# RMSNorm with GELU on one core: gamma replicated on the chip, two rows of each partition per transfer, results written in place

One NeuronCore of a Trainium2 chip. The metric is the device time of the program in microseconds, the median over several executions. All runs told here are fast, with a granted clock of 1.0.

## The reference

```python
# x: 8 x 1024 x 2048 float32, gamma: 2048 float32, eps = 1e-5
rms = np.sqrt(np.mean(x ** 2, axis=-1, keepdims=True) + eps)
out = gamma * x / rms
return 0.5 * out * (1 + np.tanh(np.sqrt(2 / np.pi) * (out + 0.044715 * out ** 3)))
```

The input and the output are 8192 rows of 8 KB, 67.1 MB each. Each row is read once and written once.

## The kernel before

A tile is 128 rows, one for each partition, 1 MB. Eight tiles make a chunk. While a chunk is loaded and its squares are summed (even tiles on ScalarE, odd ones on VectorE), the chunk ahead of it is multiplied by gamma on VectorE, sent through Gelu on ScalarE with 1/rms as the scale, and stored.

```python
P = 128
CHUNK = 8
singles = ctx.enter_context(tc.tile_pool(name="singles", bufs=1))
gamma_bc = singles.tile([P, D], fp32)
nc.gpsimd.dma_start(out=gamma_bc, in_=gamma.partition_broadcast(P))
xpool = ctx.enter_context(tc.tile_pool(name="xp", bufs=16))
ypool = ctx.enter_context(tc.tile_pool(name="yp", bufs=7))
# ... cut: pools of squares and statistics

def emit_load(i, x_tile):
    nc.sync.dma_start(out=x_tile, in_=xf[i * P:(i + 1) * P, :])

def emit_apply(i, x_tile, inv_rms, j):
    y_tile = ypool.tile([P, D], fp32)
    nc.vector.tensor_tensor(out=y_tile, in0=x_tile, in1=gamma_bc, op=ALU.mult)
    nc.scalar.activation(out=y_tile, in_=y_tile, func=AF.Gelu_apprx_tanh,
                         scale=inv_rms[:, j:j + 1])
    nc.gpsimd.dma_start(out=of[i * P:(i + 1) * P, :], in_=y_tile)
# ... cut: emit_sumsq; the loop over chunks; sqrt and reciprocal once a chunk
```

## Time and profile before

| | before |
|---|---|
| time, median | 327.62 us (326.97 to 327.99, 15 runs) |
| span of the profiled execution | 325.5 us |
| busiest engine | VectorE, 217.0 us |
| bytes moved by DMA | 135.32 MB, 416 GB/s over the span |
| transfers of 1 MB | 64 loads, 64 stores, 1 for gamma |

The times of this kernel wander between 326.8 and 328.0. That is why kernels of different sessions are compared here by their ratios to it.

### The profile page before, as it was taken

Reading aid. Unit: us, or ns where it says so; the run is one execution under the profiler, and the core shown is the slowest. Engines: PE = TensorE matmul, PEld = TensorE weight load, DVE = VectorE, ACT = ScalarE, POOL = GpSimd, SP = SyncE. Lnnn points to the kernel's source line nnn. Section 1 sums busy time; section 2 is a strip of 40 time slices with the busy share of each in tenths; the row PEclk is TensorE's granted clock in tenths of the full one; section 3 lists DMA queues with packets and bytes.
Section 4 is the critical chain, followed back from the end, with each engine's and each line's share of the span. In section 5 each row is a group of like instructions: output and inputs, shape, how many; then the busy total and the mean of one; then the engine's idle time right before and its main releaser. Section 6 shows DMA issues by size and latency. Waiting matters only on the chain.

```text
span 325.5 us, 723 instructions
## 1 busy us (share of the span) xinstructions
DVE 217.0 (67%) x137; ACT 208.1 (64%) x153; POOL 34.9 (11%) x69
## 2 busy tenths in 40 slices
DVE  0599722866667767766668768766668677699800
ACT  4230599519993139936994269925796398685940
POOL 1000012101110001110111002110111001110210
DMA  7999999999999999999999999999999999999994
GB/s 298 427 422 423 423 412 429 426 429 426 429 426 425 430 424 430 426 428 428 428 427 427 427 428 429 424 430 426 429 426 429 426 428 426 426 428 391 413 406 200
DMA packets 18582, 135.32 MB, mean 416 GB/s; under 512 B 2064, under 2 KB 2064, under 8 KB 2064
## 3 DMA queue, kind: packets, MB, share of 16 engines
q0 software_dynamic: 9360, 68.16, 49.8%
q1 hardware_dynamic: 9216, 67.11, 49.2%
q14 instruction: 6, 0.05, 0.0%
HBM read 68.16 MB, written 67.11 MB: 416 GB/s over the span
## 4 chain that ended last, share of the span: by engine, by line
issue 65%; DMA 10%; POOL 9%; DVE 6%; ACT 5%; POOLq 0%; DVEq 0%; PEldq 0%; ACTq 0%
POOL out_dram L78 9%; DMA out_dram<-y_tile 7%; DVE y_tile L73 4%; DMA gamma_bc<-in_gamma_dram 3%; ACT y_tile L74 3%; DVE sq_v L64 2%; ACT sq_s L58 1%; ACT L74 0%; ACT L108 0%; POOLq L78 0%; POOLq L145 0%; ACT rms L108 0%; DVE inv_rms L113 0%; DVE sumsq L64 0%; DVEq L73 0%
## 5 line engine op out<-in xcount | busy, mean ns | idle before, releaser
L73 DVE TENSOR_TENSOR y_tile<-x_tile,gamma_bc 128x2048 f32<-128x2048 f32 x64 | 145.7, 2290 | 88.8 <-DMA out_dram<-y_tile 73.4
L74 ACT ACTIVATE y_tile<-y_tile,inv_rms 128x2048 f32<-128x2048 f32 x64 | 124.6, 1990 | 30.3 <-DVE inv_rms L113 21.0
L64 DVE CUSTOM_DVE_ANT_0 sq_v<-x_tile 128x2048 bf16<-128x2048 f32 x32 | 73.0, 2281 | 0.0
L58 ACT ACTIVATE sq_s<-x_tile 128x2048 bf16<-128x2048 f32 x32 | 60.7, 1895 | 15.2 <-DMA x_tile<-in_x_dram 15.2
L78 POOL DMA_DIRECT2D out_dram<-y_tile x64 | 34.0, 531 | 277.5 <-ACT y_tile L74 277.5
L108 ACT ACT_TABLE_LOAD x8 | 10.3, 1283 | 47.5 <-DVE sumsq L64 47.5
L74 ACT ACT_TABLE_LOAD x8 | 10.3, 1283 | 0.1
L108 ACT ACTIVATE rms<-sumsq,eps_t 128x8 f32<-128x8 f32 x8 | 2.4, 301 | 10.8 <-DVE sumsq L64 10.7
L58 ACT ACTIVATION_READ_ACCUMULATOR sq_s<-x_tile 128x1 f32 x32 | 6.0, 186 | 0.0
L113 DVE RECIPROCAL inv_rms<-rms 128x8 f32<-128x8 f32 x8 | 1.6, 198 | 1.7 <-ACT rms L108 1.7
L64 DVE DVE_READ_ACCUMULATOR2_ANT sumsq<- 128x1 f32 x32 | 2.6, 83 | 0.0
L58 ACT ACT_TABLE_LOAD x1 | 1.3, 1283 | 0.7 <-PEq L131 0.7
L39 POOL DMA_DIRECT2D gamma_bc<-in_gamma_dram x1 | 0.7, 667 | 0.8 <-PEq L145 0.8
L41 DVE MEMSET eps_t<- 128x1 f32 x1 | 0.1, 59 | 0.8 <-PEq L131 0.8
L131 POOL MEMSET const-float32-0.0<- 128x1 f32 x1 | 0.1, 98 | 0.2 <-issue 0.2
L131 POOL MEMSET const-bfloat16-1.0<- 128x1 bf16 x1 | 0.1, 101 | 0.0
L131 POOL MEMSET const-uint8-127<- 128x1 uint8 x1 | 0.1, 99 | 0.0
L131 POOL MEMSET const-float32-1.0<- 128x1 f32 x1 | 0.1, 98 | 0.0
## 6 DMA issues: line engine op xcount, KB each, us to landing
x_tile<-in_x_dram SPq DMA_DIRECT2D x64, 1024.0 KB, 28.0
out_dram<-y_tile POOLq DMA_DIRECT2D x64, 1024.0 KB, 18.2
gamma_bc<-in_gamma_dram POOLq DMA_DIRECT2D x1, 1024.0 KB, 10.3
```

The costliest lines, as they stand in the source:

```text
L39: nc.gpsimd.dma_start(out=gamma_bc, in_=gamma.partition_broadcast(P))
L41: nc.vector.memset(eps_t, eps_f)
L58: nc.scalar.activation(out=sq_s, in_=x_tile, func=AF.Square, accum_out=sumsq[:, j:j + 1],)
L64: nc.vector.tensor_tensor_reduce(out=sq_v, in0=x_tile, in1=x_tile, scale=1.0, scalar=0.0, op0=ALU.mult, op1=ALU.add, accum_out=sumsq[:, j: ...
L73: nc.vector.tensor_tensor(out=y_tile, in0=x_tile, in1=gamma_bc, op=ALU.mult)
L74: nc.scalar.activation(out=y_tile, in_=y_tile, func=AF.Gelu_apprx_tanh, scale=inv_rms[:, j:j + 1],)
L78: nc.gpsimd.dma_start(out=of[i * P:(i + 1) * P, :], in_=y_tile)
L108: nc.scalar.activation(out=rms[:, :cn], in_=sumsq[:, :cn], func=AF.Sqrt, bias=eps_t, scale=1.0 / D,)
L113: nc.vector.reciprocal(out=inv_rms[:, :cn], in_=rms[:, :cn])
L131: nc = _bacc.Bacc("TRN2", target_bir_lowering=False, num_devices=1)
```

## The change

Its intent: to move fewer bytes and to move them in larger pieces. Gamma is read once as a row of 8 KB and replicated into PSUM by matmuls with a column of ones, in place of a broadcast load of 1 MB. A block is 256 rows, of which partition p holds rows 2p and 2p+1, contiguous in memory on both sides: 16 KB per partition, 2 MB per transfer. The results overwrite the block, so there are no y tiles; 11 blocks take the place of 16 x tiles and 7 y tiles. The multiply takes both rows at once, and only the very last block's is split.

```diff
-    CHUNK = 8
+    SUB = 2
+    CHUNK = 4
+    xb = xf.rearrange("(b p s) d -> b p s d", p=P, s=SUB)
+    ob = of.rearrange("(b p s) d -> b p s d", p=P, s=SUB)
-    gamma_bc = singles.tile([P, D], fp32)
-    nc.gpsimd.dma_start(out=gamma_bc, in_=gamma.partition_broadcast(P))
+    gamma_row = singles.tile([1, D], fp32)
+    nc.scalar.dma_start(out=gamma_row, in_=gamma.partition_broadcast(1))
+    ones = singles.tile([1, P], fp32)
+    nc.vector.memset(ones, 1.0)
+    gamma_bc = psum.tile([P, D], fp32)
+    for n in range(0, D, 512):
+        nc.tensor.matmul(gamma_bc[:, n:n + 512], ones, gamma_row[:, n:n + 512],
+                         start=True, stop=True)
-    xpool = ctx.enter_context(tc.tile_pool(name="xp", bufs=16))
-    ypool = ctx.enter_context(tc.tile_pool(name="yp", bufs=7))
+    xpool = ctx.enter_context(tc.tile_pool(name="xp", bufs=11))
-        nc.sync.dma_start(out=x_tile, in_=xf[i * P:(i + 1) * P, :])
+                blk = xpool.tile([P, SUB, D], fp32)
+                nc.sync.dma_start(out=blk, in_=xb[b])
-        nc.vector.tensor_tensor(out=y_tile, in0=x_tile, in1=gamma_bc, op=ALU.mult)
+            nc.vector.tensor_tensor(
+                out=blk, in0=blk,
+                in1=gamma_bc[:, None, :].to_broadcast([P, SUB, D]), op=ALU.mult)
+            for s in range(SUB):
+                nc.scalar.activation(
+                    out=blk[:, s, :], in_=blk[:, s, :], func=AF.Gelu_apprx_tanh,
+                    scale=inv_rms[:, 2 * j + s:2 * j + s + 1])
-        nc.gpsimd.dma_start(out=of[i * P:(i + 1) * P, :], in_=y_tile)
+        nc.gpsimd.dma_start(out=ob[b], in_=blk)
 # cut: row 0 of a block is summed on ScalarE, row 1 on VectorE; the split of the
 # last block's multiply; renamed lists and the widths of the statistics' tiles
```

More of the change, by code (lines that the diff above doesn't have):

```diff
@@ L30 @@
     N, D = xf.shape
-    assert N % P == 0
-    ntiles = N // P
-    nchunks = (ntiles + CHUNK - 1) // CHUNK
+    rows_per_block = P * SUB
+    assert N % rows_per_block == 0
+    nblocks = N // rows_per_block
+    nchunks = (nblocks + CHUNK - 1) // CHUNK
+    xb = xf.rearrange("(b p s) d -> b p s d", p=P, s=SUB)
+    ob = of.rearrange("(b p s) d -> b p s d", p=P, s=SUB)
     eps_f = float(eps)
     singles = ctx.enter_context(tc.tile_pool(name="singles", bufs=1))
-    gamma_bc = singles.tile([P, D], fp32)
-    nc.gpsimd.dma_start(out=gamma_bc, in_=gamma.partition_broadcast(P))
+    gamma_row = singles.tile([1, D], fp32)
+    nc.scalar.dma_start(out=gamma_row, in_=gamma.partition_broadcast(1))
+    ones = singles.tile([1, P], fp32)
+    nc.vector.memset(ones, 1.0)
+    psum = ctx.enter_context(tc.tile_pool(name="ps", bufs=1, space=bass.MemoryType.PSUM))
+    gamma_bc = psum.tile([P, D], fp32)
+    for n in range(0, D, 512):
+        nc.tensor.matmul(gamma_bc[:, n:n + 512], ones, gamma_row[:, n:n + 512],
+                         start=True, stop=True)
     eps_t = singles.tile([P, 1], fp32)
     nc.vector.memset(eps_t, eps_f)
-    xpool = ctx.enter_context(tc.tile_pool(name="xp", bufs=16))
-    ypool = ctx.enter_context(tc.tile_pool(name="yp", bufs=7))
+    xpool = ctx.enter_context(tc.tile_pool(name="xp", bufs=11))
     sq_s_pool = ctx.enter_context(tc.tile_pool(name="sqs", bufs=1))
@@ L47 @@
     statpool = ctx.enter_context(tc.tile_pool(name="statp", bufs=3))
-    chunk_x_tiles = {}
+    chunk_blocks = {}
     chunk_inv_rms = {}
-    def emit_load(i, x_tile):
-        nc.sync.dma_start(out=x_tile, in_=xf[i * P:(i + 1) * P, :])
-    def emit_sumsq(j, x_tile, sumsq):
-        if j % 2 == 0:
-            sq_s = sq_s_pool.tile([P, D], bf16)
-            nc.scalar.activation(
-                out=sq_s, in_=x_tile, func=AF.Square,
-                accum_out=sumsq[:, j:j + 1],
-            )
-        else:
-            sq_v = sq_v_pool.tile([P, D], bf16)
-            nc.vector.tensor_tensor_reduce(
-                out=sq_v, in0=x_tile, in1=x_tile,
-                scale=1.0, scalar=0.0,
-                op0=ALU.mult, op1=ALU.add,
-                accum_out=sumsq[:, j:j + 1],
-            )
@@ L71, in emit_apply, with emit_sumsq @@
-    def emit_apply(i, x_tile, inv_rms, j):
-        y_tile = ypool.tile([P, D], fp32)
-        nc.vector.tensor_tensor(out=y_tile, in0=x_tile, in1=gamma_bc, op=ALU.mult)
-        nc.scalar.activation(
-            out=y_tile, in_=y_tile, func=AF.Gelu_apprx_tanh,
-            scale=inv_rms[:, j:j + 1],
-        )
-        nc.gpsimd.dma_start(out=of[i * P:(i + 1) * P, :], in_=y_tile)
+    def emit_sumsq(blk, j, sumsq):
+        sq_s = sq_s_pool.tile([P, D], bf16)
+        nc.scalar.activation(
+            out=sq_s, in_=blk[:, 0, :], func=AF.Square,
+            accum_out=sumsq[:, 2 * j:2 * j + 1],
+        )
+        sq_v = sq_v_pool.tile([P, D], bf16)
+        nc.vector.tensor_tensor_reduce(
+            out=sq_v, in0=blk[:, 1, :], in1=blk[:, 1, :],
+            scale=1.0, scalar=0.0,
+            op0=ALU.mult, op1=ALU.add,
+            accum_out=sumsq[:, 2 * j + 1:2 * j + 2],
+        )
@@ new lines, in emit_apply @@
+    def emit_apply(b, blk, inv_rms, j, split_mult=False):
+        if split_mult:
+            for s in range(SUB):
+                nc.vector.tensor_tensor(
+                    out=blk[:, s, :], in0=blk[:, s, :], in1=gamma_bc,
+                    op=ALU.mult,
+                )
+                nc.scalar.activation(
+                    out=blk[:, s, :], in_=blk[:, s, :], func=AF.Gelu_apprx_tanh,
+                    scale=inv_rms[:, 2 * j + s:2 * j + s + 1],
+                )
+        else:
+            nc.vector.tensor_tensor(
+                out=blk, in0=blk,
+                in1=gamma_bc[:, None, :].to_broadcast([P, SUB, D]), op=ALU.mult
+            )
+            for s in range(SUB):
+                nc.scalar.activation(
+                    out=blk[:, s, :], in_=blk[:, s, :], func=AF.Gelu_apprx_tanh,
+                    scale=inv_rms[:, 2 * j + s:2 * j + s + 1],
+                )
+        nc.gpsimd.dma_start(out=ob[b], in_=blk)
@@ L80 @@
     for c in range(nchunks + 1):
-        cn = min(CHUNK, ntiles - c * CHUNK) if c < nchunks else 0
+        cn = min(CHUNK, nblocks - c * CHUNK) if c < nchunks else 0
         prev = c - 1
-        pn = len(chunk_x_tiles.get(prev, ()))
+        pn = len(chunk_blocks.get(prev, ()))
+        last_chunk = c == nchunks
         if cn > 0:
-            sumsq = statpool.tile([P, CHUNK], fp32)
-            x_tiles = []
+            sumsq = statpool.tile([P, 2 * CHUNK], fp32)
+            blocks = []
@@ L88 @@
             for j in range(cn):
-                i = c * CHUNK + j
-                x_tile = xpool.tile([P, D], fp32)
-                emit_load(i, x_tile)
-                x_tiles.append(x_tile)
-            chunk_x_tiles[c] = x_tiles
+                b = c * CHUNK + j
+                blk = xpool.tile([P, SUB, D], fp32)
+                nc.sync.dma_start(out=blk, in_=xb[b])
+                blocks.append(blk)
+            chunk_blocks[c] = blocks
         for j in range(max(cn, pn)):
             if cn > 0 and j < cn:
-                emit_sumsq(j, chunk_x_tiles[c][j], sumsq)
+                emit_sumsq(chunk_blocks[c][j], j, sumsq)
@@ L98 @@
             if pn > 0 and j < pn:
-                emit_apply(prev * CHUNK + j, chunk_x_tiles[prev][j],
-                           chunk_inv_rms[prev], j)
+                emit_apply(prev * CHUNK + j, chunk_blocks[prev][j],
+                           chunk_inv_rms[prev], j,
+                           split_mult=last_chunk and j == pn - 1)
         if pn > 0:
-            del chunk_x_tiles[prev]
+            del chunk_blocks[prev]
             del chunk_inv_rms[prev]
         if cn > 0:
-            rms = statpool.tile([P, CHUNK], fp32)
+            rms = statpool.tile([P, 2 * CHUNK], fp32)
@@ L108 @@
             nc.scalar.activation(
-                out=rms[:, :cn], in_=sumsq[:, :cn], func=AF.Sqrt,
+                out=rms[:, :2 * cn], in_=sumsq[:, :2 * cn], func=AF.Sqrt,
                 bias=eps_t, scale=1.0 / D,
             )
-            inv_rms = statpool.tile([P, CHUNK], fp32)
-            nc.vector.reciprocal(out=inv_rms[:, :cn], in_=rms[:, :cn])
+            inv_rms = statpool.tile([P, 2 * CHUNK], fp32)
+            nc.vector.reciprocal(out=inv_rms[:, :2 * cn], in_=rms[:, :2 * cn])
```

## The prediction

> **What bounds the kernel now.** I read the page first: the busy shares of the engines, then the DMA lines of the 40 slices.
>
> ```profile
> DVE 217.0 (67%) x137; ACT 208.1 (64%) x153; POOL 34.9 (11%) x69
> DMA  7999999999999999999999999999999999999994
> DMA packets 18582, 135.32 MB, mean 416 GB/s; under 512 B 2064, under 2 KB 2064, under 8 KB 2064
> ```
>
> No compute engine is above 67% over the span, and no slice but the first and the last shows the DMA below 90%. The 16 DMA engines are the bound. To see how exact that is I asked for stretches (columns: start:end, length, busy us of DVE, ACT and POOL, clock, DMA share, GB/s).
>
> ```profile
> 8.00:16.00 8.00, 4.42 (x2) 2.00 (x2) 0.00 (x0) 1.00 1.01 427
> 56.00:280.00 224.00, 157.22 (x100) 152.83 (x114) 25.50 (x48) 1.00 1.01 427
> 299.00:301.00 2.00, 2.00 (x2) 2.00 (x2) 0.53 (x1) 1.00 0.71 299
> 309.00:311.00 2.00, 0.00 (x0) 2.00 (x2) 0.53 (x1) 1.00 1.00 410
> 321.00:323.00 2.00, 0.00 (x0) 0.00 (x0) 0.00 (x0) 1.00 0.09 37
> 323.00:325.50 2.50, 0.00 (x0) 0.00 (x0) 0.00 (x0) 1.00 0.00 0
> ```
>
> The rate is 427 GB/s with loads alone (8 to 16 us) and with loads and stores together (56 to 280), and about 410 with stores alone (309 to 311). The share never falls but for some 1.9 us at the start (0.76 of the first 8 us), 0.6 us around 300 us, and 4.3 us after about 321.2, when the last bytes have landed. So the 325.5 us are about 318.7 us of full DMA and 6.8 us of ends and dip.
>
> The view of waits says who is held, and by what.
>
> ```profile
> DVE y_tile L73 <- DMA out_dram<-y_tile: 73.4, 41, 10.3
> ACT L108 <- DVE sumsq L64: 47.5, 7, 10.8
> DVE y_tile L73 <- DMA gamma_bc<-in_gamma_dram: 10.7, 1, 10.7
> ```
>
> VectorE waits 73.4 us for stores to free y buffers: the engines wait for the transfers. The 10.7 us for gamma are VectorE's, not the DMA's, which ran at 427 GB/s meanwhile. The chain of waits is 65% "issue" and tells little here, as the transfers form a queue that no instruction waits behind. Last, the table of transfers (KB each, median us from issue to landing) and the costs of the instructions:
>
> ```profile
> x_tile<-in_x_dram SPq DMA_DIRECT2D x64, 1024.0 KB, 28.0
> out_dram<-y_tile POOLq DMA_DIRECT2D x64, 1024.0 KB, 18.2
> q1 hardware_dynamic: 9216, 67.11, 49.2%
> L73 DVE TENSOR_TENSOR y_tile<-x_tile,gamma_bc 128x2048 f32<-128x2048 f32 x64 | 145.7, 2290 | 88.8 <-DMA out_dram<-y_tile 73.4
> L74 ACT ACTIVATE y_tile<-y_tile,inv_rms 128x2048 f32<-128x2048 f32 x64 | 124.6, 1990 | 30.3 <-DVE inv_rms L113 21.0
> ```
>
> A load takes 28 us where its own bytes take 2.46 (1.0486 MB at 427 GB/s): with half of the rate each, 28.0/4.9 = 5.7 loads and 18.2/4.9 = 3.7 stores stand in the queues. 9216 packets for 64 loads are 144 a load: 128 rows of 8 KB and 16 small ones.
>
> **What the Trainium skill says.** "DMA: Bandwidth & Descriptors", section "Where 436 GB/s comes from", gives a ceiling of 435.2 GB/s for the 16 engines; this trace holds 427, 98.1% of it. The same page, "Why small descriptors are slow (HBM only)", names a fixed cost of about 3 cycles per packet on trn2; the trace leaves room for such a cost, but doesn't prove it. The same page, "Queues, rings and completion order", says that each DMA engine takes the queues it has work for in turn, packet by packet; the 49.8% and 49.2% of the two queues agree. "VectorE: DVE Perf Modes", "The perf-mode tier table", gives fp32 tensor_tensor one element per cycle from SBUF and from PSUM alike, 2293 ns for 2048 elements; the trace has 2290 from SBUF, and nothing yet from PSUM.
>
> **The change, part by part.**
>
> *Gamma.* The broadcast of 1 MB into 128 partitions goes; one row of 8 KB and four small matmuls into PSUM replace it. As the DMA is full from 3 us on, its 1.0486 MB come off the end: 1.0486/427 = 2.46 us. The matmuls are new and no row prices them; they have until the first block is loaded and summed (2 + 4.9 + 2.3 = some 9 us), and VectorE waited until 11.6 us before anyhow. Nothing on the path.
>
> *Transfers of 2 MB in 16 KB rows.* In the built program both sides are 128 rows of 4096 contiguous floats, so I expect packets of 16 KB: 32 x 144 = 4608 on each queue, half. An 8 KB row takes 8192/(427/16) = 307 ns on its engine; at the page's ceiling it would be 301. If those 6 ns are a cost per packet, halving 1024 data packets on each engine saves 512 x 6 = 3.0 us; if they are the fabric's, nothing. I take half, 1.5 us, an estimate from that page and this trace.
>
> *Vector and scalar work.* 31 multiplies of 4096 elements replace 62 of 2048: by the 2290 ns and 0.96 GHz I estimate 2290 + 2133 = 4.42 us each, so some 5 us of VectorE disappear. A block then costs VectorE 4.4 + 2.28 + 0.08 = 6.8 us and ScalarE 1.9 + 0.19 + 2 x 1.99 = 6.1, against 9.8 us of DMA for a block in and out. All of it beside the DMA: 0.
>
> *Buffers.* 16 x tiles and 7 y tiles become 11 blocks, 22 tiles, written in place; a block is held from its load to the end of its store. Does the DMA stay fed? The multiplies still stand straight after the block's sums in the built order, ahead of the reciprocal. VectorE's chain for the first four blocks: loaded at about 7, then 3 x 6.8 + 2.3 to the last sum, about 30 us; one more multiply, then the reciprocal at 34; two Gelus of 1.99 and the first store at about 38.5 us (43.1 before). Until then only loads run, and 11 blocks last until 2 + 11 x 4.9 = 56 us, so they don't run dry. At 40 us some 7.8 blocks have landed and 3.2 are in the load queue. From there the two queues share the rate, so that number stays. The same reckoning for the kernel before gives 23 tiles less 16.5 at 45 us, 6.5, against the 5.7 read above; I trust it. Four blocks and a bit wait for their chunk, so some 3 blocks stand in the store queue. Full DMA throughout.
>
> *The tail.* After the last load (call it T) the store queue holds about 2.5 blocks, 12.7 us at 412 GB/s. Block 27's store is issued at T + 6.1 (a sum of squares and two Gelus), block 28's at T + 11.2 (last sum 2.4, multiply 4.4, reciprocal 0.2, two Gelus 4.0), then one every 4.0 us against 5.1 of transfer. No gap, so the dip of 0.6 us goes too.
>
> Sum: 327.77 - 2.46 - 0.6 - 1.5 = 323.2 us. I add 0.4 for the first rival below: 323.6.
>
> **Rivals.**
>
> *A gap in the tail.* If the store queue holds only one block at T, it is empty at T + 3, and block 27's bytes start at about T + 7.5: 4.5 us of idle DMA, and all gains but those of the packets are gone, about 327.7. For it: 2 MB stores come in lumps of two Gelus, and every chunk's first Gelu waits for the next load on ScalarE's queue. Against it: the reckoning of the queues. I give a sizeable gap about 1 in 6.
>
> *Starved loads.* In place, a load waits for a store, where before it waited for a multiply. If loads fall behind for 1 us in each of 8 chunks, the time is about 332. Against: 3 blocks of reserve, 30 us at half rate.
>
> *The packets count in full or more.* If bigger rows lift the rate to the ceiling and the stores alone from 412 too, 3 us and about 1 more come: 320.5. For: half as many completions. Against: at 98.1% of the ceiling there is little left.
>
> *PSUM as an operand slows VectorE.* Even at 7 us a multiply the block costs 9.4 us, just below the 9.8: no change in the middle, some 3 us in the tail. The page speaks against it.
>
> **Range and chances.** The gamma term is near certain (2.46); the packets give 0 to 4, the tail takes 0 to 4.5. All good: 320.5. Packets 0 and most of the gap: 327.5. So 320.6 to 327.0 for 8 in 10, at the centre 323.6. Faster by over 2% needs less than 321.2, only the packets' full worth does it: 0.14. Slower by over 2% needs more than 334.3, a starved DMA beyond what the reserve allows: 0.03. Within 2%: 0.83.
>
> **What would show it.** Right: bytes 134.3 MB; packets about 9,200 with none between 512 B and 16 KB but gamma's; share 1.0 from 3 us to the end of the stores; middle rate between 427 and 432; first store issued near 38 us; multiplies at 4.4 us; VectorE's longest wait no more for y tiles. Wrong: a middle rate below 427 (then large rows are worse, and my packet term has the wrong sign), slices below 9 in the middle (starved loads), or a dip of over 2 us some 35 us before the end (the tail's gap).

## The result, and the profile after

The kernel after takes **319.58 us** (319.37 to 319.78, 8 runs), 0.9757 of the time before (95% interval 0.9748 to 0.9766). A ratio is the mean time of one kernel's fast runs over the mean of the other's fast runs of the same rounds, so it isn't quite the ratio of the medians quoted. Predicted were 323.6 us and a range of 320.6 to 327.0. The direction was right, the size was not: 8.0 us saved where I had 4.2, and below the range.

From the page of the kernel after, busy engines, the DMA's share in slices and the packets:

```profile
PE 7.2 (2%) x8; PEld 2.5 (1%) x8; DVE 213.3 (67%) x107; ACT 209.5 (66%) x153; POOL 17.4 (5%) x36
DMA  8999999999999999999999999999999999999995
DMA packets 9223, 134.27 MB, mean 422 GB/s; under 512 B 1025, under 2 KB 1025, under 8 KB 1025
```

The DMA is still the bound and still never falls below 90% but at the ends. Bytes fell by 1.05 MB, packets by half. The same stretches as before, the last line being the end of the data (columns: start:end, length, busy us of PE, PEld, DVE, ACT and POOL, clock, DMA share, GB/s):

```profile
8.00:16.00 8.00, 2.77 (x4) 0.66 (x2) 7.30 (x4) 4.00 (x4) 0.00 (x0) 1.00 1.00 430
56.00:280.00 224.00, 0.00 (x0) 0.00 (x0) 159.51 (x80) 155.82 (x115) 12.79 (x24) 1.00 1.01 431
299.00:301.00 2.00, 0.00 (x0) 0.00 (x0) 0.00 (x0) 0.69 (x1) 0.53 (x1) 1.00 1.00 426
309.00:311.00 2.00, 0.00 (x0) 0.00 (x0) 0.00 (x0) 0.00 (x0) 0.00 (x0) 1.00 1.02 434
314.00:316.00 2.00, 0.00 (x0) 0.00 (x0) 0.00 (x0) 0.00 (x0) 0.00 (x0) 1.00 0.14 57
```

The middle runs at 431 GB/s where it ran at 427, and the stores alone at the end at some 430 where they ran at 410. There is no dip around 300 us. The data ends at about 314.3 us, and 3.6 us follow to the end of the span, where 4.3 followed before. So something was gained in four places: bytes, rate, end of the stream, and end of the program. The waits, the transfers and the multiply:

```profile
ACT sq_s L65 <- DMA blk<-in_x_dram: 81.3, 25, 6.0
DVE sq_v L70 <- DMA blk<-in_x_dram: 70.4, 22, 7.6
blk<-in_x_dram SPq DMA_DIRECT2D x32, 2048.0 KB, 25.6
out_dram<-blk POOLq DMA_DIRECT2D x32, 2048.0 KB, 34.7
L89 DVE TENSOR_TENSOR blk<-blk,gamma_bc 128x4096 f32<-128x4096 f32 x31 | 136.8, 4413 | 0.9
```

Both engines now wait for loads, VectorE no longer for stores to free a y tile: the same shortage of DMA time, seen from the other side.

### The profile page after: what moved, and what is told of

It reads as the page before. It is cut to its first block, busy times and chain, and to the rows that moved or that the text cites.

```text
span 317.9 us, 555 instructions
## 1 busy us (share of the span) xinstructions
PE 7.2 (2%) x8; PEld 2.5 (1%) x8; DVE 213.3 (67%) x107; ACT 209.5 (66%) x153; POOL 17.4 (5%) x36
## 4 chain that ended last, share of the span: by engine, by line
issue 63%; DMA 21%; POOL 4%; ACT 3%; DVE 2%; ACTq 1%; POOLq 0%; DVEq 0%; SPq 0%
DMA out_dram<-blk 11%; DMA blk<-in_x_dram 11%; POOL out_dram L98 4%; ACT blk L94 2%; DVE blk L89 1%; DVE sq_v L70 1%; ACTq L167 1%; ACT L94 0%; ACT L130 0%; POOLq L98 0%; POOLq L167 0%; ACT rms L130 0%; ACT sq_s L65 0%; DVEq L89 0%; SPq L112 0%
## 5 line engine op out<-in xcount | busy, mean ns | idle before, releaser
L89 DVE TENSOR_TENSOR blk<-blk,gamma_bc 128x4096 f32<-128x4096 f32 x31 | 136.8, 4413 | 0.9
L70 DVE CUSTOM_DVE_ANT_0 sq_v<-blk 128x2048 bf16<-128x2048 f32 x32 | 73.2, 2287 | 70.5 <-DMA blk<-in_x_dram 70.4
L94 ACT ACTIVATE blk<-blk,inv_rms 128x2048 f32<-128x2048 f32 x62 | 120.2, 1988 | 0.1
L65 ACT ACTIVATE sq_s<-blk 128x2048 bf16<-128x2048 f32 x32 | 61.0, 1906 | 81.3 <-DMA blk<-in_x_dram 81.3
L98 POOL DMA_DIRECT2D out_dram<-blk x32 | 17.2, 537 | 282.9 <-ACT blk L94 274.5
L50 PE MATMUL gamma_bc<-gamma_row,ones 1*128 1x512 f32 x8 | 7.2, 1072 | 3.6 <-DMA gamma_row<-in_gamma_dram 3.6
L65 ACT ACTIVATION_READ_ACCUMULATOR sq_s<-blk 128x1 f32 x32 | 6.0, 186 | 0.0
L80 DVE TENSOR_TENSOR blk<-blk,gamma_bc 128x2048 f32<-128x2048 f32 x2 | 4.4, 2260 | 0.0
L84 ACT ACTIVATE blk<-blk,inv_rms 128x2048 f32<-128x2048 f32 x2 | 3.9, 1986 | 0.0
L50 PEld LDWEIGHTS gamma_bc<-gamma_row,ones 1*128 1x128 f32 x8 | 2.5, 325 | 6.7 <-issue 6.7
## 6 DMA issues: line engine op xcount, KB each, us to landing
blk<-in_x_dram SPq DMA_DIRECT2D x32, 2048.0 KB, 25.6
out_dram<-blk POOLq DMA_DIRECT2D x32, 2048.0 KB, 34.7
```

What stands on the lines that cost most here:

```text
L50: nc.tensor.matmul(gamma_bc[:, n:n + 512], ones, gamma_row[:, n:n + 512], start=True, stop=True)
L65: nc.scalar.activation(out=sq_s, in_=blk[:, 0, :], func=AF.Square, accum_out=sumsq[:, 2 * j:2 * j + 1],)
L70: nc.vector.tensor_tensor_reduce(out=sq_v, in0=blk[:, 1, :], in1=blk[:, 1, :], scale=1.0, scalar=0.0, op0=ALU.mult, op1=ALU.add, accum_out ...
L80: nc.vector.tensor_tensor(out=blk[:, s, :], in0=blk[:, s, :], in1=gamma_bc, op=ALU.mult,)
L84: nc.scalar.activation(out=blk[:, s, :], in_=blk[:, s, :], func=AF.Gelu_apprx_tanh, scale=inv_rms[:, 2 * j + s:2 * j + s + 1],)
L89: nc.vector.tensor_tensor(out=blk, in0=blk, in1=gamma_bc[:, None, :].to_broadcast([P, SUB, D]), op=ALU.mult)
```

## The experiments

Fourteen kernels ran, in four sessions, each beside the kernel before on the same chip. All gave correct results. A packet is here what the profile records as one: each contiguous row of a partition is a packet, and each transfer has 16 more of 4 B that report its completion. A transfer has landed when the last of these is in. Theory one, from the prediction: each data packet has a fixed cost on its DMA engine, and I had credited half of it. Theory two: each transfer has a cost, in the stream or at an end. The rival to both: buffers and schedule made the rate.

| run | what it is | median us | ratio to before |
|---|---|---|---|
| e1_gamma_only | before, gamma by matmul | 324.38 | 0.9913 |
| e4_1mb_8kb | after, transfers of 1 MB, rows of 8 KB | 324.68 | 0.9924 |
| e3_2mb_8kb | after, transfers of 2 MB, rows of 8 KB | 321.96 | 0.9839 |
| after | transfers of 2 MB, rows of 16 KB | 319.58 | 0.9757 |
| e2_gamma_dma | after, gamma by broadcast load | 322.48 | 0.9854 |
| e5_1mb_4kb | after, transfers of 1 MB, pieces of 4 KB | 329.61 | 1.0082 |
| e7_no_split | after, last multiply whole | 319.53 | 0.9756 |
| e8_32kb | transfers of 4 MB, rows of 32 KB | 319.83 | 0.9781 |
| e9_act_stores | after, stores on ScalarE's queue | 328.86 | 1.0051 |
| e10_32kb_act | both of these | 335.41 | 1.0250 |
| e11_swapped | after, loads from GpSimd, stores from sync | 319.74 | 0.9763 |
| e12_1mb_8kb_swapped | e4 with the same exchange | 323.83 | 0.9887 |
| e13_before_swapped | before with the same exchange | 324.99 | 0.9925 |
| e14_swapped_first8 | e11, first 8 loads from sync | 319.16 | 0.9756 |
| e15_swapped_first2 | e11, first 2 loads from sync | 318.61 | 0.9739 |

The first four rows are a ladder from the kernel before to the kernel after, one part changed at each step (the kernel after ran in another session than the three others). By the ratios, and 327.3 us for the kernel before: gamma 2.85 us, in-place blocks and all of the schedule -0.36, fewer transfers 2.78, longer rows 2.68; in all 7.95. The intervals of the ratios are about 0.4 us wide on either side.

### Gamma alone, on either kernel

e1 takes the gamma lines of the diff into the kernel before and nothing else. e2 undoes them in the kernel after:

```diff
-    gamma_bc = psum.tile([P, D], fp32)      # row load, ones, four matmuls
+    gamma_bc = singles.tile([P, D], fp32)
+    nc.gpsimd.dma_start(out=gamma_bc, in_=gamma.partition_broadcast(P))
```

> The kernel before, with only the gamma part of the change: a row of 8 KB and four matmuls into PSUM in place of the broadcast of 1 MB; transfers stay 1 MB in 8 KB rows. If gamma is worth its bytes, 1.0486 MB at 427 GB/s, the time falls by 2.5 us (ratio 0.9925), the middle stays at 427 GB/s and the stores alone at the end stay near 412. If the earlier gamma also lets the first stores start earlier and that counts, it falls by more than 3 us. If the gamma load was hidden, it doesn't fall.

> The kernel after, with only the gamma part undone (broadcast of 1 MB by DMA, gamma in SBUF). If the parts add up, it is 2.4 us above the kernel after (some 322.0 us), with a middle rate of 431 GB/s still. If gamma was the cause of the higher rates, it goes back towards 325 or more and 427 GB/s. The multiply of 4096 elements from SBUF alone should take 4.42 us as from PSUM.

e1 saves 2.6 us by the medians and 2.85 by the ratio; e2 loses 2.9. The bytes are worth 2.46 and the rest is small: the part adds up and stands by itself. The DMA rates in the slices of the page show the rest, kernel before and then e1:

```profile
GB/s 298 427 422 423 423 412 429 426 429 426 429 426 425 430 424 430 426 428 428 428 427 427 427 428 429 424 430 426 429 426 429 426 428 426 426 428 391 413 406 200
```

```profile
GB/s 299 426 423 422 401 430 428 425 428 429 426 425 431 426 426 429 428 426 427 431 425 426 429 426 428 429 427 428 426 429 426 427 428 428 426 426 430 427 425 162
```

In e1 the stores alone at the end run at 425 to 430, with the same 1 MB transfers that ran at 391 to 413 in the kernel before. So the slow end of the kernel before was no property of stores, as I had read it. Its own trace says so too: the last load's packets end before 280 us, and the stores alone still ran at full rate until the dip.

```profile
290.00:294.00 4.00, 4.00 (x4) 3.34 (x4) 0.53 (x1) 1.00 1.01 426
310.00:314.00 4.00, 0.00 (x0) 2.65 (x2) 1.06 (x2) 1.00 1.03 416
```

There the store queue ran dry once, at 300 us; in e1 the first store is issued at 34.9 us, not 43.1, the queue is deeper to the end, and it never runs dry. In the packet records of the trace the 8 KB packets of the kernel before take 309 ns from 282 to 300 us and 320 ns on average from 302 us on; in e1 they take 310 from 308 us on, and in e13 below, whose stores don't run dry either, 309. That it is the dry spell which left the engines slower is what the traces suggest; no run took only that away.

### Size of the transfer and size of the row

e4 and e3 keep the kernel after's buffers, gamma and engines. e4 moves a block in two transfers, one for each row of a partition; e3 takes rows p and 128+p into a block, so that one transfer of 2 MB is made of 256 rows of 8 KB.

```diff
 # e4: 1 MB transfers, 8 KB rows (stores alike)
-                nc.sync.dma_start(out=blk, in_=xb[b])
+                for s in range(SUB):
+                    nc.sync.dma_start(out=blk[:, s, :], in_=xb[b][:, s, :])
 # e3: 2 MB transfers, 8 KB rows (ob alike)
-    xb = xf.rearrange("(b p s) d -> b p s d", p=P, s=SUB)
+    xb = xf.rearrange("(b s p) d -> b p s d", p=P, s=SUB)
 # e5: 1 MB transfers, 4 KB pieces (stores alike)
-                nc.sync.dma_start(out=blk, in_=xb[b])
+                for h in range(0, D, D // 2):
+                    nc.sync.dma_start(out=blk[:, :, h:h + D // 2],
+                                      in_=xb[b][:, :, h:h + D // 2])
```

> The kernel after, with 2 MB transfers still (64 in all), but each of 256 rows of 8 KB and not 128 of 16 KB: a block takes rows p and 128+p, no longer 2p and 2p+1. Theory one, a cost per packet: 512 more packets on each DMA engine at 5.9 ns, 3.0 us more than the kernel after (322.6), middle rate back to 427 to 428. Theory two, a cost per transfer (its 16 completion packets and turnarounds): same as after, 319.6, rate 431.

> The kernel after, with each block moved by two transfers of 1 MB in 8 KB rows (128 transfers in all), layout and buffers as after. Theory one, a cost per packet: as the run with 2 MB in 8 KB rows, 322.6 or a little more. Theory two, a cost per transfer: 3 us more than the 2 MB run, so 322.6 where the 2 MB one is at 319.6. If both count, 2 MB in 8 KB rows lies between. If it stays at 319.6, neither matters, and the in-place buffers or the schedule made the rate.

> The kernel after with twice the suspected packet cost: each block in two transfers of 1 MB (as the run with 1 MB in 8 KB rows, 324.7), but of 256 pieces of 4 KB. Packets so far took 309 ns for 8 KB and 611 for 16 KB in the steady stretch, so 302 ns per 8 KB and a fixed 7 ns. Packet theory: a 4 KB packet takes 158 ns, and 1024 more of them on each DMA engine cost 4.9 us (at the 4.8 ns a packet that the time showed between 8 and 16 KB) to 7.2 us (at 7 ns): 329.6 to 331.9. If only the number of transfers counts, it stays at 324.7.

e3 lies at 321.96, between the two theories, and e4 at 324.68: both count, by almost the same amount. (A transfer of e4 takes every second row of memory, one of e3 takes whole neighbouring rows; the packets took 309 ns in both, so that didn't slow them.) The rival is out: e4, with the in-place blocks and the kernel after's schedule but the old transfers, is 0.3 us slower than e1. e5, with twice e4's data packets, costs 4.9 us more, just what was expected at 4.8 ns for each of 1024 packets per engine. In the total that is partly luck: e5's last landing comes 7.1 us after e4's, and its end is 2.1 us shorter (table below). The steady stretch is the better witness: 427.1 against 420.6 GB/s before rounding is 4.85 us over all the bytes, 4.7 ns a packet. Most of the other 2.3 us are a later start, with 1.5 MB moved by 8 us and not 2.3.

The middle of each run, from 70 to 280 us, in the order e5, e4, e3, after (a fence each; last columns DMA share and GB/s):

```profile
70.00:280.00 210.00, 0.00 (x0) 0.00 (x0) 141.60 (x71) 140.01 (x102) 30.47 (x44) 1.00 1.03 421
```

```profile
70.00:280.00 210.00, 0.00 (x0) 0.00 (x0) 141.10 (x70) 140.88 (x104) 22.85 (x43) 1.00 1.01 427
```

```profile
70.00:280.00 210.00, 0.00 (x0) 0.00 (x0) 143.84 (x72) 141.25 (x104) 15.78 (x22) 1.00 1.01 428
```

```profile
70.00:280.00 210.00, 0.00 (x0) 0.00 (x0) 145.65 (x72) 143.15 (x105) 11.73 (x22) 1.00 1.01 431
```

The rate follows the packet: 421, 427, 428, 431. The trace records every packet with its duration, and in the steady stretch nearly all of one size take the same time:

```
packet size      4 B (completion)   4 KB   8 KB   16 KB   32 KB
median, ns       9                  159    309    611     1213
two halves less one whole, ns              9      7       9
```

A fixed 7 to 9 ns stands in each packet. In the time, 512 packets fewer on each engine brought 2.4 us (321.96 to 319.58), or 4.7 ns each: less than 7 to 9, perhaps because packets of the two queues overlap a little on an engine (the DMA share is over 1, 1.01 and in e5 1.03).

The transfers' 2.7 us, e4 to e3, are only in small part in the middle: 427 and 428 differ by 0.7 us over the whole span (0.55 before rounding). I took the last landing and the end of the program from the traces. GpSimd, which issues the stores, ends with a drain instruction (it starts at the last issue and ends only after the last landing), which the views don't count as busy:

```
run                   transfers from   last landing   drain ends after   last landing
                      GpSimd           us             last landing, us   to end, us
before                65               322.02         2.70               3.48
e1_gamma_only         64               318.99         2.66               3.44
e4_1mb_8kb            64               319.26         2.66               3.44
e3_2mb_8kb            32               318.34         1.36               2.15
after                 32               315.74         1.35               2.13
e2_gamma_dma          33               318.14         1.39               2.16
e8_32kb               16               317.25         0.70               1.47
e5_1mb_4kb            64               326.40         0.50               1.38
```

From e4 to e3 the last landing comes 0.92 us earlier, of which 64 completion packets of 9 ns on each engine are 0.58; and from the last landing to the end takes 1.29 us less. Together that is 2.2 us, the distance of the two spans. Most of the other 0.5 lies outside the spans (time less span is 2.1 us in e4, 1.75 in e3), and I have no cause for it. The drain grows with the number of transfers that GpSimd issued, 41 to 44 ns each. One row does not fit: e5, with 64 transfers of 256 pieces, drains in 0.50 us. Its issues take 737 ns each where those of e4 take 531, but e3's take 717 and its drain fits; so I have no cause for it.

GpSimd is not alone at the end. SyncE passes its own waits for all the transfers, and in every row the program ends 0.77 to 0.81 us after the later of the two. SyncE had passed its last wait 0.07 us after the last landing in the kernel before, 0.57 in e4, 1.02 in the kernel after: the drain was the later one in each row but e5, where SyncE was (0.57). So the drain's cost is what it has beyond SyncE, in the kernel after 0.33 us and not 1.35.

### The split of the last multiply

> The kernel after without the one part left: the last block's multiply is not split in two. The last store's bytes start only when the four blocks ahead of it have been stored, so the split should be worth nothing: 319.5, the same within 0.2 us. If the end hangs on the last Gelu, it is some 2 us slower.

319.53 against 319.58: worth nothing, as expected. The stores of the last four blocks stand in line.

### Longer rows still

e8 takes four rows per partition: 32 KB rows, 4 MB transfers, 6 blocks.

```diff
-    SUB = 2
-    CHUNK = 4
+    SUB = 4
+    CHUNK = 2
-    xpool = ctx.enter_context(tc.tile_pool(name="xp", bufs=11))
+    xpool = ctx.enter_context(tc.tile_pool(name="xp", bufs=6))
 # squares, multiplies and Gelus as before, two rows at a time; gamma's row in two
 # halves; the last multiply is not split
```

> The change carried further: four rows of each partition in one block (4 MB transfers, 32 KB rows, 6 blocks, chunks of two blocks, gamma loaded in two halves to save memory), multiplies still of 4096 elements. Packet theory: 1215 ns a packet, 256 packets fewer per engine, 1.2 to 1.8 us; transfers halve once more: 0.3 us in the stream, and GpSimd's drain after the last landing, 2.7 us with 64 or 65 transfers on its queue and 1.35 with 32, becomes 0.7: 317 to 317.5 in all against 319.6. If 4 MB blocks leave a gap at the end (a store goes out only after four Gelus, 8 us) or late first stores starve the loads, it is 320 or more.

It comes to 319.83 (319.23 to 320.80), no faster than the kernel after. Stretches of e8, whose profiled run was the slowest of the four, 320.80:

```profile
60.00:120.00 60.00, 0.00 (x0) 0.00 (x0) 42.69 (x22) 41.55 (x30) 1.60 (x3) 1.00 1.01 422
120.00:280.00 160.00, 0.00 (x0) 0.00 (x0) 110.84 (x55) 106.82 (x81) 4.25 (x8) 1.00 1.00 434
285.00:300.00 15.00, 0.00 (x0) 0.00 (x0) 6.39 (x3) 14.94 (x11) 1.06 (x2) 1.00 0.95 409
300.00:308.00 8.00, 0.00 (x0) 0.00 (x0) 0.00 (x0) 3.40 (x2) 0.53 (x1) 1.00 0.92 393
```

The packet theory holds in the calm stretch: 434 GB/s, and 1213 ns a packet as expected. The gain goes back in two places. After the first stores come (60 to 120 us) the rate is 422, with the DMA busy all the while and packets of up to 2539 ns: (434 - 422)/434 of 60 us is 1.7 us. At the end the share falls to 0.92 to 0.95, the gap that had been the rival: 0.05 of 15 and 0.08 of 8 us are 1.4 us. Together 3.1 us bring the expected 317 to 317.5 to about the time of that run; the two faster runs of e8 (319.2 and 319.3) must have lost less. The slow packets all lie before 90 us; why they are slow stays open.

### Where the stores are issued from

The drain is a cost of GpSimd's transfers, so I took them away from it.

```diff
 # e9, on the kernel after
-        nc.gpsimd.dma_start(out=ob[b], in_=blk)
+        nc.scalar.dma_start(out=ob[b], in_=blk)
 # e10: the same edit on e8
```

> The kernel after, with the 32 stores issued from ScalarE's queue in place of GpSimd's, nothing else. Theory: the drain of GpSimd at the end (1.35 us after the last landing with 32 transfers on its queue, 2.7 with 64) is a cost of its own transfers and disappears: 318.2 us, with the same packets of 611 ns. Rival: the drain is a fixed end of the program, 319.6. Third: ScalarE's in-order queue, which now waits for transfers' semaphores shared with the loads, holds up the Gelus and makes it slower, above 320.5.

> The 32 KB rows with the stores on ScalarE's queue, both changes at once, in search of the fastest version. If they add up, 316.3 to 316.8 us: 0.7 us below the 32 KB run alone, since only its 16 stores' drain goes away. If the shared semaphores hold ScalarE, slower than the 32 KB run.

Both are slower, 328.86 and 335.41, and e9 tells nothing of the drain's worth: the scheduler put the program together differently. In its trace 57 of VectorE's 107 instructions stand at another place than in the kernel after, multiplies among them. The waits of e9 show what came of it:

```profile
ACT blk L94 <- DVE inv_rms L135: 86.3, 6, 21.6
```

ScalarE sits idle for 86.3 us until the reciprocals come, stores come late, and from 270 us on the DMA is not full. The end alone is of use: 1.46 us from last landing to end in place of 2.13.

The next try exchanges the two queues and leaves the order of the three compute engines as it was, which I checked in the built programs of e11 and the kernel after (their traces agree).

```diff
 # e11 on the kernel after, e12 on e4, e13 on the kernel before
-                nc.sync.dma_start(out=blk, in_=xb[b])
+                nc.gpsimd.dma_start(out=blk, in_=xb[b])
-        nc.gpsimd.dma_start(out=ob[b], in_=blk)
+        nc.sync.dma_start(out=ob[b], in_=blk)
```

> The kernel after with the two queues exchanged: loads issued from GpSimd, stores from the sync engine; the built order of the vector, scalar and tensor engines is unchanged (the run with stores on ScalarE's queue was not: its multiplies had moved). In the traces so far GpSimd drains for 1.35 us after the last store has landed where it issued 32 stores, 2.7 us where it issued 64. If that drain is a cost of its transfers and ends earlier when they are loads, landed some 35 us before the end, the program gets 1.35 us shorter: 318.2 (319.5 for the kernel after). If the end of the program costs that anyway, 319.5. If loads suffer from GpSimd's issue, above 320.

> The 1 MB transfers in 8 KB rows of the kernel after's layout (324.7 us; 2.7 above the same with 2 MB transfers), with the queues exchanged in the same way. If half of those 2.7 us was GpSimd's drain of 64 stores, the drain's 2.7 us go and it comes to 322.0; the rest of the distance to the exchanged 2 MB, 16 KB version is then packets (2.4) and completions in the stream (about 1).

> The kernel before with the queues exchanged and nothing else (gamma still broadcast by GpSimd, ahead of the loads). If GpSimd's drain of 65 transfers (2.7 us after the last landing) goes, 327.0 - 2.7 = 324.3. If gamma's broadcast now lies ahead of the loads in the same queue, VectorE starts earlier and the first store too, and the dip of the kernel before at 300 us may close: up to 1.4 us more, 322.9. If the drain is no cost of its transfers, 327.0.

The kernel before gains 2.5 us from this alone (324.99), e4 0.85 by the medians and 1.2 by the ratios, the kernel after nothing (319.74). In all three traces GpSimd's drain now ends over 34 us before the last landing, and from there to the end it takes 0.89, 1.34 and 1.33 us. So the drain left the path each time, and e11 must have lost as much elsewhere. The drain itself is no shorter: it ends 3.15, 3.14 and 1.71 us after the last packet of GpSimd's own queue, as it does without the exchange (3.05, 3.01 and 1.68). It belongs to GpSimd's transfers, loads or stores. What is left at the end is SyncE's: its last wait is passed 0.09 us after the last landing in e13, 0.52 in e12 and e11. In e13 the dip at 300 us has closed as well, but its stream starts 0.9 us later, and its last landing is still 0.2 us later than in the kernel before: the gain is the drain's. The times of the first packet of x, the bytes moved by 8 us, the last landing and the end, from the traces:

```
run                   first x packet, us   MB by 8 us   last landing, us   landing to end   span
after                 1.74                 2.16         315.74             2.13             317.86
e11_swapped           2.64                 1.85         316.50             1.33             317.84
e15_swapped_first2    1.74                 2.17         315.49             1.26             316.75
```

GpSimd's first load moves 0.9 us later (it is issued at 1.25 us and not 0.74, and takes 1.4 us to its first packet and not 1.0), and 0.32 MB are missing by 8 us, 0.74 us at 431 GB/s: the last landing is 0.76 later. (The 0.25 us that I name in the expectation below were gamma's row and not x.) e12 starts as late, 2.64 us against 1.75 in e4; that explains some 0.8 us of the 1.3 by which its last landing is later, and I have not found the rest. If the late start is the cause in e11, early loads on the sync engine's queue should give it back.

```diff
 # e14; e15 with b < 2
-                nc.gpsimd.dma_start(out=blk, in_=xb[b])
+                (nc.sync if b < 8 else nc.gpsimd).dma_start(out=blk, in_=xb[b])
```

> Stores on the sync engine's queue and loads on GpSimd's, but the first 8 loads issued from the sync engine, where the first bytes came 0.25 us earlier and the first 8 us moved more. Theory: in the run with all loads on GpSimd the drain's 0.8 us at the end were gained (2.13 us from last landing to the end became 1.33) and lost again to a later start (0.76 us later last landing). With the start restored both count: 318.7 against 319.5. Rival: the last landing was later for another reason, and it stays at 319.5 or above. The built order of the vector engine's multiplies shifts by one place, which can blur it.

> The same with only the first two loads from the sync engine. If the lost start lies in the first transfers alone, 318.7 as well; if GpSimd's generation of all early loads is slow, between 318.7 and 319.7.

e15 takes 318.61 us (318.51 to 319.02), 0.9739 of the kernel before. That is 1.0 us below the kernel after by the medians and 0.6 by the ratios, whose intervals overlap (0.9724 to 0.9754, and 0.9748 to 0.9766); the two did not run side by side. Its trace has the start of the kernel after, and 1.26 us from the last landing to the end. A cancellation, then, and the lowest time of all. e14 reaches 319.16; its last landing is as early (315.56) but the end took 1.80 us. There SyncE passed its last wait 0.96 us after the last landing, in e15 0.43: it paused for 0.41 us between two waits, where in e15 each follows the last within 0.06. The kernel after has such a pause too (0.43), behind the drain; what makes it is not known. In both runs the order of VectorE and ScalarE also shifted at some places; the middle stayed at 431 GB/s.

## Why the prediction was wrong

It was wrong in one step, and there in two terms; the other terms of the sum held. Three smaller slips stand at the end of the list.

- **What bounds the kernel:** right. The DMA stayed full from 4 us to the end of the stores.
- **Gamma, 2.46 us and the dip of 0.6:** right in sum, 2.85 us in e1. The matmuls ran from 3.6 to 10.8 us and the first multiply started at 11.0, 0.15 us after VectorE was free; nothing of it on the path:

```profile
3.61 7.16 PE L50 MATMUL gamma_bc<-gamma_row,ones 1*128 1x512 f32 x8 [3.61 <-DMA gamma_row<-in_gamma_dram]
11.00 4.42 DVE L89 TENSOR_TENSOR blk<-blk,gamma_bc 128x4096 f32<-128x4096 f32 x1
```

- **Vector and scalar work, 0:** right. The multiply of 4096 elements with gamma in PSUM takes 4413 ns, predicted 4420, and 4416 with gamma in SBUF (e2), so the rival of a slow PSUM operand is out, as the Trainium skill's "VectorE: DVE Perf Modes", "The perf-mode tier table", had it. (The 0.96 GHz of the prediction is the clock in that page's first table; the second 2048 elements took 4413 - 2290 = 2123 ns where 2133 were reckoned.)
- **Buffers, 0:** right (e1 to e4, -0.36 us). First store at 40.2 us, predicted 38.5. Loads took 25.6 us and stores 34.7, which at 9.7 us for a block in and out is 2.6 and 3.6 blocks in the queues; predicted 3.2 and some 3.
- **The tail, no gap:** right. The last block's sums start at 275.7; block 27's store goes out 6.1 us later, as predicted, block 28's 12.9 later where I had 11.2, and the queue was deep enough.
- **"Transfers of 2 MB in 16 KB rows", 1.5 us: this is the step that failed.** Two terms. First, the packets: I worked out 3.0 us from 6 ns a packet and took half, because the trace of before could not tell a packet's cost from the fabric's. The runs show 2.4 to 2.7 us; the full figure was the better one, as the rival "the packets count in full or more" had it. That rival even named half as many completions, without a sum for them. Second, and larger: the number of transfers has no term of its own in my sum. Halving it is worth 2.7 to 2.8 us (e4 to e3): 0.9 in the stream, 1.3 in GpSimd's drain after the last landing, and 0.5 that no trace explains. I had counted the 4.3 us from last data to end as fixed, and never asked why a program needs them. In the records of the trace of before, though not in its views, the drain stood to be seen.
- **The allowance of 0.4 for a gap:** nothing came of it.
- **Slips that did not decide the result:** "about 410 with stores alone" was read from a stretch after the dip; before the dip they ran at 426 to 428. A gap of 4.5 us would have eaten all gains, the packets' too: 323.2 + 4.5 is 327.7. And the equal shares of the two queues are no test of the engines' taking turns, since each queue moves 67 or 68 MB in any case.

In place of my 4.2 us (3.06 for gamma and dip, 1.5 for packets, less 0.4) the runs have 7.95 by the ratios: 2.85, 2.7 for packets, 2.8 for transfers, less 0.36. The range was too narrow at the low end for the same reason: its 320.5 "all good" case had packets and a faster end for the stores in it, and no transfers.

## What to carry to other kernels

Where the DMA is full from end to end, count three things apart: bytes, packets (each row of a partition that is contiguous on both sides is one) and transfers; here each of the three was worth 2.4 to 2.9 us of 327. Then look at the microseconds after the last landing and ask which engine is still at work there: an engine that issued the last transfers may have a bill that grows with their number, and giving it the loads, which end earlier, takes the bill off the path. What that gains is only the distance to the next engine still at work. A larger transfer is not better without end: at 4 MB the lumps cost what the packets gained.

## What the Trainium skill lacked or had wrong

- "DMA: Bandwidth & Descriptors", "Why small descriptors are slow (HBM only)": this section names about 3 cycles per packet, as a matter of small descriptors. If these are cycles of the 850 MHz that the page gives for the fabric, that is an estimated 3.5 ns; the packet records show 7 to 9 ns, at every size from 4 to 32 KB, and from 8 to 16 KB it was still worth 2.4 us of 322.
- The same page, "Issuing engines are not separate DMA queues", says that issuing from several engines at once saves only the sequencer's time, usually small, and that the transfers run on the same DMA engines whoever issued them. Which engine issues matters all the same: here stores from GpSimd cost a drain of 42 ns per transfer after the last landing (2.70 us for 65, 1.35 for 32, 0.70 for 16; one run with 64 transfers of 256 pieces had 0.50), and the exchange of the queues alone took 2.5 us off the kernel before. No page that I read has a drain that grows with GpSimd's transfers.
- The same page, "Specifications", gives a first byte after about 1 us on GpSimd's path and 0.6 on the other. It does not say from where it counts. From the start of the issuing instruction to the first packet the runs show 1.4 us (e11, 1.25 to 2.64) and 1.0 (kernel after, 0.74 to 1.74), the distance of 0.4 the same; from that instruction's end, 0.72 and 0.63. Where loads from SyncE had been issued first, GpSimd's first packet came 4.2 us (gamma in the kernel before) and 4.4 us (e15) after the start of its issue.
- No page that I read says that a stream of stores stays slower after its queue has run dry, which the kernel before suggests: 8 KB packets of 320 ns on average after the dip, 309 before it, and 310 at the end of e1, where it never ran dry.
